# An encoder trunk in float32 halves: up-projections of eight in eleven chunks by seven block products, F tiles in three portions

## The chip, the cores and the metric

One core of a Trainium2 chip. The metric is the device time of one execution in microseconds (us); runs of one kernel lie within 0.1% of each other here. The engines are TensorE (PE; its weight loads are shown apart as PEld), VectorE (DVE), ScalarE (ACT), GpSimd (POOL) and SyncE (SP), which issues the loads of weights.

## What is computed

Two layers of an encoder over 512 tokens with a model width D of 1024. Each layer is an FFN, a token mixer (attention in a window, a pool over windows, gates) and another FFN. All is float32. The change is in the FFN:

```python
def swiglu(u, w1, w3, w2):
    return (jax.nn.silu(u @ w1) * (u @ w3)) @ w2
...
        h = h + 0.5 * swiglu(rms_norm(h, ffn1_norm[l]), ffn1_w1[l], ffn1_w3[l], ffn1_w2[l])
```

`w1` and `w3` are 1024 x 2816, `w2` is 2816 x 1024. So an FFN has K = 8 tiles of 128 in its two up-projections and 22 tiles of 128 hidden columns ("F tiles"), which come in 11 chunks of 256 columns.

## The kernel before

x lies with D on the partitions and the tokens along the free axis. A product keeps float32's bits by three parts: each operand is split into a high half (an exact copy in a shorter form, by ACT) and a low half (the difference, by DVE), and `mm3` adds high x high, high x low and low x high. Every part is a matmul of its own with its own weight load.

Weights come in pieces of 512 KB ([128, 1024] in SBUF): `do_load` lets SP fetch a piece into `raw` (3 buffers), `do_split` makes `wh` on ACT (L157) and `wl` on DVE (L158; 3 buffers each). Loads run four pieces ahead of use, splits two.

An FFN (`ffn`) goes through its F tiles in two portions, `HALVES = ((0, 12), (12, 22))`. For each chunk of 256 columns `pair` makes the products with `w1` and then with `w3`, over 8 K tiles, 2 column tiles, and 3 parts, each matmul with all 512 tokens as its moving columns: 96 matmuls. Then come `gate` (L376 to L380) and `gated` (L386), and `split_sb` splits the hidden tile for the down-projection. The inverse root of the norm, `r`, isn't in the operand `us`, so that the products may begin before it is known; `gate` multiplies it in twice. After each portion the down-projection runs over the portion's F tiles, four pairs of output tiles, and `residual` adds them to x (L359).

In the mixer attention is cut into small steps between the products of the gates: scores (L630, L631), softmax, transposes of probabilities (L677), their split (L679 on ACT, L680 on DVE), values (L693, L694). At the very end `natural` transposes x (L426) and `closing` makes the last down-projection with the tokens on the partitions.

The order on each engine is set by a scheduler from the program's order, its data and its buffers; PSUM has 8 banks of [128, 512], handed out in turn.

Of the kernel before, what the change touches and what calls it, by code (L numbers as in the profile page):

```python
# [38 lines left out]
PAD = 16  # L39
NEG = -1e30  # L40
LEAST = -3e38
KC = 4
HALVES = ((0, 12), (12, 22))
# [4 lines left out]
# Column layout of the packed vectors: the norm gains, biases, scales and sinks of each  # L48
# layer, and tables that depend on shapes alone.
# [22 lines left out]
def encoder_kernel(ctx, tc, x, vec, gfin, w1a, w3a, w2a, w_in, pool_w, w_ba, w_bp, w_out, w1b, w3b, w2b, out):  # L72
# [3 lines left out]
    act = ctx.enter_context(tc.tile_pool(name="act", bufs=56))  # L76
# [14 lines left out]
    def slot(dt=F32, n=512):  # L91
        return act.tile([P, n], dt, tag="slot", name=uniq("slot"))
# [22 lines left out]
    # the tensor engine's clock rises while the first data come in  # L115
# [16 lines left out]
    specs = []  # L132
    held = set()  # pieces that stay until the end, in slots of their own
    state = {"load": 0, "split": 0, "use": 0}
    raws, parts = {}, {}
    LOAD_AHEAD, SPLIT_AHEAD = 4, 2

    def piece(parts_of):
        specs.append(parts_of)

    def do_load(i):
        raw = wp.tile([P, 1024], F32, tag="raw", name=uniq("raw"), bufs=3)
        for lo, hi, shape, src in specs[i]:
            k, c = shape
            nc.sync.dma_start(out=raw[lo:hi, : k * c].rearrange("p (k c) -> p k c", k=k), in_=src)
        raws[i] = raw

    def do_split(i):
        raw = raws.pop(i)
        k, c = specs[i][0][2]  # L150
        n = k * c
# [3 lines left out]
        wh = wp.tile([P, 1024], F32R, tag="wh", name=uniq("wh"), bufs=3)  # L155
        wl = wp.tile([P, 1024], F32R, tag="wl", name=uniq("wl"), bufs=3)
# [7 lines left out]
    def ahead():  # L164
        while state["load"] < min(len(specs), state["use"] + LOAD_AHEAD):
            do_load(state["load"])
            state["load"] += 1
        while state["split"] < min(len(specs), state["use"] + SPLIT_AHEAD):
            do_split(state["split"])
            state["split"] += 1  # L170
# [17 lines left out]

    def plan_ffn(w1, w3, w2, first, last):
        for f0, f1 in HALVES:  # L190
            for c in range(f0 // 2, f1 // 2):
                if first and c == 0:
# [6 lines left out]
            if last and f0:  # L199
                for k0, k1 in ((f0, f1 - KC), (f1 - KC, f1)):  # L200
                    for e in range(2):
                        for k, n in ksteps(k0, k1, 2):
                            piece(wsrc(w2, k, n, e * 512, 512))
                            if k1 == f1:
                                held.add(len(specs) - 1)
# [36 lines left out]
    def pair(us, k0=0, k1=KD, between=None):  # L242
        """Two output tiles (256 columns of the weights) over the K tiles of `us`."""
# [13 lines left out]
    def turned(ps, half):  # L257
        """The transpose of an exact half."""
        nc.tensor.matmul(ps, lhsT=half, rhs=identr, start=True, stop=True)  # L259

    def split_sb(src, hi=None, lo=None):
        hi = slot(F32R) if hi is None else hi
        lo = slot(F32R) if lo is None else lo
# [11 lines left out]
    class Norm:  # L275
        """Sum of squares over the model dimension, tile by tile, then its inverse root."""
# [17 lines left out]
        def root(self, r, total, n):  # L294
            """r = (total / D + eps) ** -0.5, with a Newton step on the table's root."""
# [9 lines left out]
        def rows(self):  # L305
            """The inverse root of each token along the free axis, on every partition."""
# [7 lines left out]
        def cols(self):  # L314
            """The inverse root of each token on its partition, [P, NT]."""
# [526 lines left out]
```

## Time and profile before

| | |
|---|---|
| timed runs | 1999.99 us (median of 3; 1999.25 to 2000.25) |
| profiled execution, span from first to last instruction | 1997.6 us |
| what lies around the span, by the median of the runs | 2.4 us |
| matmuls | 9053 |
| busy: PE, DVE, ACT, POOL | 99%, 55%, 36%, 2% |
| DMA | 189.56 MB, mean 95 GB/s |

The profiled execution's own time isn't listed apart from the timed runs; its span is, and the runs' median stands beside it. A share of busy time is the union of an engine's instructions over the span; matmuls overlap each other, so PE's share says little by itself, and the distance between starts of equal matmuls says more. Idle time of an engine matters only where another one waits for its result.

### The profile page before, as it was taken

The numbers are of one execution on the slowest core, as the hardware profiler recorded it, in microseconds if no ns is written. First come the engines' busy times: TensorE is split into PE (matmuls) and PEld (weight loads), VectorE is DVE, ScalarE is ACT, GpSimd is POOL, SyncE is SP. The second block draws the span as 40 slices with busy tenths as digits, with TensorE's granted clock in tenths as the row PEclk, the third lists the DMA queues.
The fourth block names the chain that finished last, engine by engine and source line by source line (L and its number), as shares of the span: only waits on it lengthen the run. The fifth ranks groups of instructions, "written<-read, shape, count | busy, mean of one in ns | idle before, by whom it ended". The sixth has DMA issues, their size and how long they took to land.

```text
span 1997.6 us, 22600 instructions
## 1 busy us (share of the span) xinstructions
PE 1984.4 (99%) x9053; PEld 1650.2 (83%) x9053; DVE 1089.3 (55%) x1705; ACT 713.3 (36%) x1091; POOL 41.0 (2%) x48
## 2 busy tenths in 40 slices
PE   9999999999999999999999999999999999999998
PEld 7888888888888888888888888888888888888886
DVE  5753454477765654355456434545777647544444
ACT  4321233445553332222333212334466433222333
POOL 2000000020000000000000000000200000000000
PEclk9999999999999999999999999999999999999999
DMA  5333332322233233332333333333222333333332
GB/s 176 95 95 97 101 98 85 106 85 69 74 87 104 84 107 95 95 98 93 95 95 106 95 97 100 91 98 90 80 85 64 105 96 95 95 95 95 106 95 74
DMA packets 183467, 189.56 MB, mean 95 GB/s; under 512 B 6208, under 2 KB 176320, under 8 KB 183360
## 3 DMA queue, kind: packets, MB, share of 16 engines
q1 hardware_dynamic: 182496, 186.67, 31.6%
q8 instruction: 71, 1.16, 0.2%
q10 hardware_dynamic: 864, 1.43, 0.2%
q14 instruction: 36, 0.29, 0.0%
HBM read 185.98 MB, written 2.10 MB: 94 GB/s over the span
## 4 chain that ended last, share of the span: by engine, by line
PE 98%; ACT 0%; DVE 0%; issue 0%; ACTq 0%
PE bank L238 32%; PE bank L240 32%; PE bank L239 32%; PE bank L677 1%; PE bank L693 0%; PE bank L259 0%; PE bank L694 0%; PE bank L630 0%; PE bank L631 0%; ACT wh L157 0%; PE bank L426 0%; PE bank L308 0%; PE bank L309 0%; PE bank L320 0%; ACT tmp L460 0%; ACT slot L467 0%
## 5 line engine op out<-in xcount | busy, mean ns | idle before, releaser
L238 PE MATMUL bank<-slot,wh 128*128 128x512 f32 x2616 | 1024.0, 392 | 1.7 <-ACT wh L157 1.4
L240 PE MATMUL bank<-slot,wl 128*128 128x512 f32 x2616 | 1017.9, 389 | 2.3 <-DVE wl L158 2.3
L239 PE MATMUL bank<-slot,wh 128*128 128x512 f32 x2616 | 1018.6, 389 | 0.0
L157 ACT ACTIVATE wh<-raw 128x1024 fp32r<-128x1024 f32 (+1 forms) x356 | 368.4, 1035 | 1126.8 <-PE bank L239 786.8
L158 DVE TENSOR_TENSOR wl<-raw,wh 128x1024 fp32r<-128x1024 f32 (+1 forms) x356 | 427.6, 1201 | 483.8 <-ACT wh L157 482.8
L240 PEld LDWEIGHTS bank<-slot,wl 128*128 128x128 f32 x2616 | 491.0, 188 | 106.4 <-DVE wl L158 3.1
L238 PEld LDWEIGHTS bank<-slot,wh 128*128 128x128 f32 x2616 | 491.1, 188 | 102.1 <-ACT wh L157 3.8
L239 PEld LDWEIGHTS bank<-slot,wh 128*128 128x128 f32 x2616 | 491.3, 188 | 97.5
L386 DVE TENSOR_TENSOR tmp<-bank,tmp 128x512 f32<-128x512 f32 x88 | 60.0, 690 | 88.1 <-PE bank L240 88.1
L376 DVE TENSOR_TENSOR tmp<-bank,rrow 128x512 f32<-128x512 f32 x88 | 59.6, 690 | 83.9 <-PE bank L240 83.7
L379 DVE TENSOR_TENSOR tmp<-tmp,tmp 128x512 f32<-128x512 f32 x88 | 60.1, 687 | 23.6 <-ACT tmp L378 23.6
L265 DVE TENSOR_TENSOR slot<-tmp,slot 128x512 fp32r<-128x512 f32 x96 | 64.6, 704 | 6.2 <-ACT slot L264 6.2
L264 ACT ACTIVATE slot<-tmp 128x512 fp32r<-128x512 f32 x96 | 55.5, 617 | 22.2 <-DVE tmp L386 13.0
L238 PE MATMUL bank<-wh,slot 128*128 128x512 f32 (+1 forms) x176 | 61.8, 351 | 0.0
L240 PE MATMUL bank<-wh,slot 128*128 128x512 f32 (+1 forms) x176 | 61.7, 350 | 0.0
L239 PE MATMUL bank<-wl,slot 128*128 128x512 f32 (+1 forms) x176 | 61.7, 350 | 0.0
L359 DVE SCALAR_TENSOR_TENSOR x<-bank,x 128x512 f32<-128x512 f32 x56 | 38.2, 690 | 42.5 <-PE bank L240 42.5
L380 DVE TENSOR_TENSOR tmp<-tmp,rrow 128x512 f32<-128x512 f32 x88 | 60.2, 687 | 1.3
L378 ACT ACTIVATE tmp<-tmp 128x512 f32<-128x512 f32 x88 | 51.2, 618 | 17.1 <-DVE tmp L376 17.1
L654 ACT ACTIVATE s<-s,nm 128x256 f32<-128x256 f32 (+1 forms) x64 | 35.2, 551 | 30.2 <-DVE nm L649 30.0
L272 DVE SCALAR_TENSOR_TENSOR slot<-x,vt,slot 128x512 fp32r<-128x512 f32 x48 | 40.4, 845 | 1.6 <-ACT slot L271 1.6
L240 PEld LDWEIGHTS bank<-wh,slot 128*128 128x128 f32 x176 | 33.3, 189 | 4.4
(124 smaller groups left out, 969.9 us busy)
## 6 DMA issues: line engine op xcount, KB each, us to landing
raw<-in_ffn_w_dram SPq DMA_DIRECT2D x254, 512.0 KB, 3.7
raw<-in_w_in_dram SPq DMA_DIRECT2D x52, 512.0 KB, 3.8
raw<-in_w_out_dram SPq DMA_DIRECT2D x16, 512.0 KB, 3.5
raw<-in_ffn_w_dram SPq DMA_DIRECT2D x20, 256.0 KB, 2.9
raw<-in_w_branch_pool_dram SPq DMA_DIRECT2D x8, 512.0 KB, 3.5
raw<-in_w_branch_attn_dram SPq DMA_DIRECT2D x16, 256.0 KB, 4.0
x<-in_x_dram SPq DMA_DIRECT2D x8, 256.0 KB, 4.9
out_dram<-slot SPq DMA_DIRECT2D x4, 256.0 KB, 2.1
```

Of the source, the lines that this page charges most:

```text
L157: nc.scalar.activation(wh[:, :n], raw[:, :n], AF.Copy)
L158: nc.vector.tensor_tensor(out=wl[:, :n], in0=raw[:, :n], in1=f(wh[:, :n]), op=ALU.subtract)
L238: nc.tensor.matmul(ps, lhsT=lh, rhs=rh, start=start, stop=False)
L239: nc.tensor.matmul(ps, lhsT=lh, rhs=rl, start=False, stop=False)
L240: nc.tensor.matmul(ps, lhsT=ll, rhs=rh, start=False, stop=stop)
L264: nc.scalar.activation(hi, src, AF.Copy)
L265: nc.vector.tensor_tensor(out=lo, in0=src, in1=f(hi), op=ALU.subtract)
L376: nc.vector.tensor_tensor(out=a, in0=p[t], in1=r, op=ALU.mult)
L378: nc.scalar.activation(s, a, AF.Sigmoid)
L379: nc.vector.tensor_tensor(out=a, in0=a, in1=s, op=ALU.mult)
L380: nc.vector.tensor_tensor(out=a, in0=a, in1=r, op=ALU.mult)
L386: nc.vector.tensor_tensor(out=ta[t], in0=p[t], in1=ta[t], op=ALU.mult)
```

## The change

In the first portion, now 6 F tiles (3 chunks), a chunk is computed as before. In the other two, 8 tiles (4 chunks) each, a chunk's two up-projections are taken together as one 2 x 2 block product: weights in blocks (`w1`, `w3`) x (lower, upper half of K), tokens in two halves of 256. By Winograd's form of Strassen's scheme seven products of blocks stand for eight; each is over 4 K tiles with 256 moving columns. Sums of weight blocks are made on DVE (`combine` in `plan_seven`), sums of operand blocks once an FFN (`factors`), with the norm's `r` and gain multiplied in, so that `silu` needs no `r`. The seven products (`seven`) share three PSUM banks: ACT copies a bank out (`kept`), and a later product adds to what is in it. All three portions' down-projections are as before, of 6, 8 and 8 K tiles. Buffers are laid out anew: `raw` has 9, `wh` and `wl` 4 each, `act` 23 of 4 KB in place of 56 of 2 KB; in the mixer the scores lie in a `raw` buffer and a `tmp`. The transposes of x at the end (`natural`) stand together before `closing`.

```diff
-HALVES = ((0, 12), (12, 22))
+LEAD = 9
+PORTIONS = ((0, 6), (6, 14), (14, 22))
...
+    def plan_seven(w1, w3, c0):
...
+        event(i - 8, fetch, "21", w3, 0)
+        event(i - 8, fetch, "22", w3, KC)
+        event(i - 7, fetch, "11", w1, 0)
+        event(i - 6, fetch, "12", w1, KC)
+        event(i - 4, combine, "s3", "11", ALU.subtract, "21")
+        event(i - 3, combine, "21", "21", ALU.add, "22")
+        event(i - 3, ready, 0, "11")
+        event(i - 2, combine, "11", "11", ALU.subtract, "21")
+        event(i - 1, ready, 1, "12")
+        event(i, ready, 2, "11")
+        event(i, combine, "12", "12", ALU.add, "11")
+        event(i + 1, ready, 3, "21")
+        event(i + 2, ready, 4, "s3")
+        event(i + 3, ready, 5, "12")
+        event(i + 4, ready, 6, "22")
...
+        for f0, f1 in PORTIONS:
+            last = f1 == KF
+            gs = []
+            for c in range(f0 // 2, f1 // 2):
+                if f0:
+                    seven(forms, gs)
...
+                else:
+                    ta = gate(pair(us, between=steps))
+                    gated(pair(us, between=steps), ta, gs)
...
+    def factors(g, r):
...
+            nc.vector.scalar_tensor_tensor(
+                out=b[n][:, k % KC * HT : (k % KC + 1) * HT], in0=xs[k][:, c], scalar=col(g, k), in1=r[:, c],
+                op0=ALU.mult, op1=ALU.mult,
+            )
...
+        def ready(n):
+            src, hi, lo = b.pop(n), big(), big()
+            nc.scalar.activation(hi, src, AF.Copy)
+            nc.vector.tensor_tensor(out=lo, in0=src, in1=f(hi), op=ALU.subtract)
...
+    def seven(forms, gs):
...
+            for k in range(KC):
+                for t in range(2):
+                    c = slice(t * P, (t + 1) * P)
+                    o = ps[:, t * HT : (t + 1) * HT]
+                    last = k == KC - 1
+                    nc.tensor.matmul(
+                        o, lhsT=wh[:, k, c], rhs=bh[:, k, :], start=start and k + t == 0, stop=False, skip_group_check=True
+                    )
+                    nc.tensor.matmul(o, lhsT=wh[:, k, c], rhs=bl[:, k, :], start=False, stop=False, skip_group_check=True)
+                    nc.tensor.matmul(o, lhsT=wl[:, k, c], rhs=bh[:, k, :], start=False, stop=last, skip_group_check=True)
+
+        def kept(ps):
+            v = tmp()
+            nc.scalar.activation(v, ps, AF.Copy)
+            return v
...
+        x, y, z = bank(), bank(), bank()
+        product(x, "11", True)
+        p1 = kept(x)
+        product(z, "21", True)
+        a1 = tmp()
+        nc.vector.tensor_tensor(out=a1, in0=z, in1=p1, op=ALU.add)
+        silu(a1)
+        product(x, "t2", False)
+        u2 = kept(x)
+        product(y, "t1", True)
+        p5 = kept(y)
+        product(x, "12", False)
+        u3 = kept(x)
+        b2 = p5
+        nc.vector.tensor_tensor(out=b2, in0=u3, in1=p5, op=ALU.add)
+        product(y, "22", False)
+        a2 = u2
+        nc.vector.tensor_tensor(out=a2, in0=y, in1=u2, op=ALU.add)
+        silu(a2)
+        product(x, "t4", False)
+        nc.vector.tensor_tensor(out=a1, in0=x, in1=a1, op=ALU.mult)
+        hidden(0, a1)
+        nc.vector.tensor_tensor(out=b2, in0=b2, in1=a2, op=ALU.mult)
+        hidden(1, b2)
```

Three places show how the order moves; rows are in the order in which an engine takes them, with the changed kernel's own line numbers in its rows.

**DVE in a chunk.** Before, in the first FFN's first portion (L158 splits a weight piece, L376 to L386 gate, L265 splits a hidden tile; one more L265 and L158 end the chunk's 14 rows):

```order
L376 TENSOR_TENSOR tmp_158_875<-bank_150_813,rrow_74_404 128x512
L376 TENSOR_TENSOR tmp_160_881<-bank_151_814,rrow_74_404 128x512
L379 TENSOR_TENSOR tmp_158_875<-tmp_158_875,tmp_159_877 128x512
L158 TENSOR_TENSOR wl_166_892<-raw_152_815,wh_165_891 128x1024
L380 TENSOR_TENSOR tmp_158_875<-tmp_158_875,rrow_74_404 128x512
L379 TENSOR_TENSOR tmp_160_881<-tmp_160_881,tmp_161_883 128x512
L380 TENSOR_TENSOR tmp_160_881<-tmp_160_881,rrow_74_404 128x512
L158 TENSOR_TENSOR wl_169_922<-raw_155_845,wh_168_921 128x1024
L386 TENSOR_TENSOR tmp_158_875<-bank_162_887,tmp_158_875 128x512
L386 TENSOR_TENSOR tmp_160_881<-bank_163_888,tmp_160_881 128x512
L158 TENSOR_TENSOR wl_178_964<-raw_164_889,wh_177_963 128x1024
L265 TENSOR_TENSOR slot_171_951<-tmp_158_875,slot_170_950 128x512
```

In the changed kernel, the end of a chunk of its second portion (L196 splits a weight block, L238 is a sum of weight blocks, L598 to L606 and L575 gate, L582 splits a hidden tile):

```order
L238 TENSOR_TENSOR raw_206_1172<-raw_206_1172,raw_197_1128 128x1024
L196 TENSOR_TENSOR wl_227_1363<-raw_210_1204,wh_226_1362 128x1024
L598 TENSOR_TENSOR tmp_219_1295<-tmp_224_1330,tmp_219_1295 128x512
L238 TENSOR_TENSOR raw_210_1204<-raw_210_1204,raw_206_1172 128x1024
L601 TENSOR_TENSOR tmp_215_1263<-bank_202_1165,tmp_215_1263 128x512
L196 TENSOR_TENSOR wl_236_1406<-raw_206_1172,wh_235_1405 128x1024
L575 TENSOR_TENSOR tmp_215_1263<-tmp_215_1263,tmp_225_1359 128x512
L604 TENSOR_TENSOR tmp_211_1230<-bank_201_1164,tmp_211_1230 128x512
L606 TENSOR_TENSOR tmp_219_1295<-tmp_219_1295,tmp_215_1263 128x512
L196 TENSOR_TENSOR wl_240_1439<-raw_197_1128,wh_239_1438 128x1024
L582 TENSOR_TENSOR big_200_1163<-tmp_211_1230,big_199_1162 128x2x256
L582 TENSOR_TENSOR big_200_1163<-tmp_219_1295,big_199_1162 128x2x256
```

A chunk has gone from 14 rows (4 of 1024 columns) to 20 (11 of 1024: 7 splits and 4 sums); the gating rows L598, L601, L604 and L606 stand among splits and sums that belong to the next chunk.

**ACT in a chunk.** Before, at the same place (L157 copies a piece's high half, L378 is the sigmoid, L264 a hidden tile's high half):

```order
L157 ACTIVATE wh_156_847<-raw_143_773 128x1024
L157 ACTIVATE wh_165_891<-raw_152_815 128x1024
L378 ACTIVATE tmp_159_877<-tmp_158_875 128x512
L378 ACTIVATE tmp_161_883<-tmp_160_881 128x512
L157 ACTIVATE wh_168_921<-raw_155_845 128x1024
L157 ACTIVATE wh_177_963<-raw_164_889 128x1024
L264 ACTIVATE slot_170_950<-tmp_158_875 128x512
L264 ACTIVATE slot_172_955<-tmp_160_881 128x512
```

In the changed kernel (L195 copies a block's high half, L569 is `kept`, the copy of a bank, L574 the sigmoid):

```order
L195 ACTIVATE wh_213_1235<-raw_187_1031 128x1024
L569 ACTIVATE tmp_207_1198<-bank_201_1164 128x512
L195 ACTIVATE wh_216_1265<-raw_179_966 128x1024
L574 ACTIVATE tmp_212_1232<-tmp_211_1230 128x512
L195 ACTIVATE wh_220_1297<-raw_167_908 128x1024
L569 ACTIVATE tmp_215_1263<-bank_201_1164 128x512
L195 ACTIVATE wh_222_1302<-raw_206_1172 128x1024
L569 ACTIVATE tmp_219_1295<-bank_202_1165 128x512
L195 ACTIVATE wh_226_1362<-raw_210_1204 128x1024
L569 ACTIVATE tmp_224_1330<-bank_201_1164 128x512
L195 ACTIVATE wh_235_1405<-raw_206_1172 128x1024
L574 ACTIVATE tmp_225_1359<-tmp_215_1263 128x512
```

Each copy of a bank stands behind the copy of a weight block, and the one ahead of `tmp_225_1359`'s sigmoid reads a sum that DVE makes.

**PE in the mixer.** The values of the third head in the first layer, with what each row waits for. Before:

```order
L693 MATMUL bank_736_3914<-slot_692_3761,slot_492_2927 128x256 [waits DVE_49]
L694 MATMUL bank_736_3914<-slot_693_3762,slot_492_2927 128x256
L693 MATMUL bank_736_3914<-slot_695_3768,slot_492_2927 128x256
L694 MATMUL bank_736_3914<-slot_696_3769,slot_492_2927 128x256
L693 MATMUL bank_736_3914<-slot_698_3782,slot_492_2927 128x384
L694 MATMUL bank_736_3914<-slot_699_3783,slot_492_2927 128x384
L693 MATMUL bank_736_3914<-slot_701_3796,slot_492_2927 128x384
L694 MATMUL bank_736_3914<-slot_702_3797,slot_492_2927 128x384
```

And now (L894 and L895 are L693 and L694 of before; `big` holds the probabilities of one or two blocks of keys):

```order
L894 MATMUL bank_762_4662<-big_728_4519,big_549_3706 128x256 [waits DVE_49,Activation_49]
L895 MATMUL bank_762_4662<-big_728_4519,big_549_3706 128x256
L894 MATMUL bank_762_4662<-big_728_4519,big_549_3706 128x256 [waits Activation_49]
L895 MATMUL bank_762_4662<-big_728_4519,big_549_3706 128x256
L894 MATMUL bank_762_4662<-big_731_4537,big_549_3706 128x384 [waits Activation_49]
L895 MATMUL bank_762_4662<-big_731_4537,big_549_3706 128x384
L894 MATMUL bank_762_4662<-big_733_4550,big_549_3706 128x384 [waits Activation_49]
L895 MATMUL bank_762_4662<-big_733_4550,big_549_3706 128x384
```

Before, the row of values waits once, for DVE; now four of its rows wait for ACT's copy as well. Over the eight heads of a layer 14 of the 32 first rows of a block waited for ACT, and 25 do now.

## Rows read from the trace of the kernel before

**Rows 1.** The page: busy time, share, xinstructions by engine; granted clock in slices
```profile
PE 1984.4 (99%) x9053; PEld 1650.2 (83%) x9053; DVE 1089.3 (55%) x1705; ACT 713.3 (36%) x1091; POOL 41.0 (2%) x48
...
PEclk9999999999999999999999999999999999999999
```

**Rows 2.** The page: the chain that ended last, by engine and line
```profile
PE 98%; ACT 0%; DVE 0%; issue 0%; ACTq 0%
PE bank L238 32%; PE bank L240 32%; PE bank L239 32%; PE bank L677 1%; PE bank L693 0%; PE bank L259 0%; PE bank L694 0%; PE bank L630 0%; PE bank L631 0%; ACT wh L157 0%; PE bank L426 0%; PE bank L308 0%; PE bank L309 0%; PE bank L320 0%; ACT tmp L460 0%; ACT slot L467 0%
```

**Rows 3.** Timeline of PE: start us, us, line, out<-in, form, count
```profile
632.73 0.39 PE L240 MATMUL bank<-slot,wl 128*128 128x512 f32 x1
...
662.20 0.39 PE L238 MATMUL bank<-slot,wh 128*128 128x512 f32 x1
```

**Rows 4.** Timeline of PE in the k/v projection, 256 columns
```profile
392.75 0.28 PE L238 MATMUL bank<-wh,slot 128*128 128x256 f32 x1
...
403.79 0.28 PE L240 MATMUL bank<-wh,slot 128*128 128x256 f32 x1
```

**Rows 5.** Timeline of PE's weight loads (PEld) in the k/v projection
```profile
399.84 0.19 PEld L238 LDWEIGHTS bank<-wh,slot 128*128 128x128 f32 x1
399.96 0.19 PEld L239 LDWEIGHTS bank<-wl,slot 128*128 128x128 f32 x1
```

**Rows 6.** Busy time in the stretch of the k/v projection
```profile
core 0: us, PE busy (x) PEld busy (x) DVE busy (x) ACT busy (x) POOL busy (x), PEclk, DMA share, GB/s
392.30:403.90 11.60, 11.60 (x98) 11.60 (x98) 9.54 (x42) 8.51 (x19) 0.15 (x2) 1.00 0.24 65
```

**Rows 7.** Timeline of DVE, back to back
```profile
66.23 0.69 DVE L386 TENSOR_TENSOR tmp<-bank,tmp 128x512 f32<-128x512 f32 x1
66.83 1.22 DVE L158 TENSOR_TENSOR wl<-raw,wh 128x1024 fp32r<-128x1024 f32 x1
67.97 0.69 DVE L265 TENSOR_TENSOR slot<-tmp,slot 128x512 fp32r<-128x512 f32 x1
```

**Rows 8.** Groups by line: xcount | busy us, mean ns | idle before
```profile
L158 DVE TENSOR_TENSOR wl<-raw,wh 128x1024 fp32r<-128x1024 f32 x334 | 410.6, 1229 | 481.4 <-ACT wh L157 480.5
L157 ACT ACTIVATE wh<-raw 128x1024 fp32r<-128x1024 f32 x334 | 354.5, 1061 | 1092.0 <-PE bank L239 756.2 <-issue 296.1 <-PE bank L240 34.2
...
L386 DVE TENSOR_TENSOR tmp<-bank,tmp 128x512 f32<-128x512 f32 x88 | 60.0, 690 | 88.1 <-PE bank L240 88.1
...
L378 ACT ACTIVATE tmp<-tmp 128x512 f32<-128x512 f32 x88 | 51.2, 618 | 17.1 <-DVE tmp L376 17.1
...
L272 DVE SCALAR_TENSOR_TENSOR slot<-x,vt,slot 128x512 fp32r<-128x512 f32 x48 | 40.4, 845 | 1.6 <-ACT slot L271 1.6
...
L679 ACT ACTIVATE slot<-bank 128x384 fp32r<-128x384 f32 x32 | 14.7, 490 | 3.5 <-PE bank L677 2.6 <-PE bank L259 0.7
...
L428 ACT ACTIVATE slot<-bank 128x512 f32<-128x512 f32 x8 | 4.3, 584 | 0.0
```

**Rows 9.** Timeline of all engines, around a read of a finished PSUM bank
```profile
75.30 0.39 PE L240 MATMUL bank<-slot,wl 128*128 128x512 f32 x1
...
75.73 0.69 DVE L386 TENSOR_TENSOR tmp<-bank,tmp 128x512 f32<-128x512 f32 x1 [1.08 <-PE bank L240]
```

**Rows 10.** Timeline of ACT, back to back (row two: two instructions)
```profile
76.18 1.06 ACT L157 ACTIVATE wh<-raw 128x1024 fp32r<-128x1024 f32 x1 [3.81 <-PE bank L239]
77.15 1.14 ACT L264 ACTIVATE slot<-tmp 128x512 fp32r<-128x512 f32 x2
```

**Rows 11.** Waits: engine, line <- waited for: us in total, times, longest us
```profile
PEld bank L238 <- ACT wh L157: 3.8, 5, 1.8
...
PE bank L240 <- DVE wl L158: 2.3, 2, 1.3
...
PEld bank L693 <- ACT slot L679: 0.4, 2, 0.2
```

**Rows 12.** Busy time in the first layer's mixer (columns as in Rows 6)
```profile
369.70:670.30 300.60, 300.59 (x1479) 254.10 (x1479) 193.35 (x412) 144.42 (x272) 14.59 (x18) 1.00 0.30 87
```

More of the change, by code (lines that the diff above doesn't have):

```diff
@@ L39 @@
 PAD = 16
+HT = S // 2
+ACTS = 23
+RAWS = 9
+SPLITS = 4
 NEG = -1e30
@@ L162, in do_split, with upto @@
         )
[L164 to L170, printed above, removed]
+    def upto(i):
+        while state["event"] <= i:
+            for fn, args in events.pop(state["event"], []):
+                fn(*args)
+            state["event"] += 1
     def weights():
         i = state["use"]
-        ahead()
+        upto(i)
         state["use"] += 1
-        ahead()
         return parts.pop(i)
@@ L198, in plan_ffn @@
                 plan_pair(w3, c * 256)
-            if last and f0:
+            if last and f1 == KF:
                 for k0, k1 in ((f0, f1 - KC), (f1 - KC, f1)):
@@ L330, in encoder_kernel @@
         if k % 2 == 0:
-            while state["load"] < (2, 2, 3, 3)[k // 2]:
-                do_load(state["load"])
-                state["load"] += 1
+            for i in range((2, 2, 3, 3)[k // 2]):
+                do_load(i, uses[i])
     def opening():
@@ L342, in opening @@
                 if j == 0:
-                    ahead()
+                    upto(state["use"])
             w = [weights(), weights()]
@@ L387, in gated @@
                 gs.append(split_sb(ta[t]))
-        for hf, (f0, f1) in enumerate(HALVES):
-            last = hf == len(HALVES) - 1
+        for f0, f1 in PORTIONS:
+            last = f1 == KF
             gs = []
             for c in range(f0 // 2, f1 // 2):
-                if c == 0:
+                if f0:
+                    seven(forms, gs)
+                elif c == 0:
                     late = ups or [pair(us), pair(us)]
-                    continue
-                pa = pair(us)
-                if late:
+                elif c == 1:
+                    pa = pair(us)
                     norm.split()
@@ L400, in ffn @@
                     gated(late[1], gate(late[0]), gs)
-                    late = []
-                ta = gate(pa)
-                gated(pair(us), ta, gs)
-                if last and gain is None and c - f0 // 2 < NT:
-                    natural(c - f0 // 2)
+                    ta = gate(pa)
+                    gated(pair(us), ta, gs)
+                    forms, steps = factors(g, r)
+                else:
+                    ta = gate(pair(us, between=steps))
+                    gated(pair(us, between=steps), ta, gs)
             if last and gain is None:
+                for t in range(NT):
+                    natural(t)
                 closing(gs, f0, f1)
@@ L411, in ffn @@
             for d in range(KD // 2):
-                ps = pair(gs, f0, f1)
+                ps = pair(gs, f0, f1, None if f0 else steps)
+                if not f0 and d == KD // 2 - 1:
+                    steps(True)
                 for t in range(2):
@@ L516, in mixer @@
                     mm3(pk[t][:, :256], uh[:, c], ul[:, c], wh[:, j, :], wl[:, j, :], first, last)
-        kn = slot()
-        vs = [slot(F32R) for _ in range(KVH)]
+        kn = tmp()
+        vs = two()
         for t in range(NT):
```

176 lines of the change are left out of this document (134 added, 42 removed).

## The prediction

> **What bounds the kernel now.** Read the busy shares first: TensorE (PE) is busy 99% of the span, VectorE (DVE) 55%, ScalarE (ACT) 36%, and the clock digit is 9 in every slice, so the granted clock is at its upper level (2.4 GHz) throughout [rows 1]. A busy PE isn't yet a bound PE, because its matmuls are pipelined. So read the chain that ended last next: 98% of it is PE, and the three lines of `mm3` carry 96% [rows 2]. PE waits for almost nothing, so what the change does to the time is what it does to the spacing and number of matmuls, plus whatever waits it puts in. Spacing is read from starts, not from durations, which overlap (0.39 us each): 131 matmuls with 512 columns start from 632.73 to 662.20, so (662.20 - 632.73)/130 = 226.7 ns [rows 3]. The kernel already has a stretch of 256-column matmuls, the k/v projection: 93 of them from 392.75 to 403.79, or (403.79 - 392.75)/92 = 120.0 ns [rows 4].
>
> **Matmuls.** A chunk had 96 matmuls of 512 columns: 96 x 226.7 ns = 21.76 us. It gets 7 products x 4 K tiles x 2 tiles x 3 parts = 168 of 256 columns: 168 x 120.0 ns = 20.16 us. An eighth of the chunk would be 2.72 us; 1.60 is left, because half the columns cost more than half the time (120.0 against 113.4 ns). Eight chunks in each of four FFNs: 32 x 1.60 = **51.3 us saved**. The rest of the matmuls keep their number: a third portion only cuts the same 22 K tiles of the down-projection otherwise.
>
> What could spoil the 120 ns is the weight load, since a load is now needed every 120 ns and takes 0.19 us [rows 5]. In the k/v stretch loads take the same 0.19 us and yet start 0.12 us apart, side by side with each other and with the matmuls [rows 5], while DVE was busy for 9.54 and ACT for 8.51 of 11.60 us [rows 6], so neither loads nor other engines' traffic stretched the spacing there. I take 120.0 ns. The Trainium skill, in "TensorE: Matmul & The Clock Gate" (Part 3, The mechanism), says that a weight load overlaps matmuls in flight only when its row group differs; these loads take all rows, so by that rule the loads would stand in line, and the sum would turn into a large loss (a rival below). The rows speak against it.
>
> **VectorE.** In steady state a chunk had 4 splits of 1024 columns and 10 operations of 512; by the new order it has 7 splits and 4 sums of 1024, and 9 of 512. What one occupies is again start to start: 0.60 us for 512 columns, from PSUM too, and 1.14 for 1024 [rows 7]. So 4 x 1.14 + 10 x 0.60 = 10.6 us before and 11 x 1.14 + 9 x 0.60 = 17.9 us now, of 20.16. The upper bound is full durations, 11 x 1.229 + 9 x 0.690 = 19.7 us [rows 8]. Either fits, closely. The cover is the lead: with four split buffers the split of a product may begin when the product four back is done, and is needed three products (3 x 24 x 0.120 = 8.6 us) later. About 1.5 us of this is the copy and subtraction themselves, some queueing goes off too; I count two products, 5.8 us. A portion is four chunks, so DVE could fall 1.4 us behind in each, to 21.6 us a chunk, before PE waits. Then the down-projection (192 x 0.2267 = 43.5 us, with 8 splits and 8 residuals, 13.9 us) lets it recover. Cost taken: 0.
>
> **The factors of each FFN** are 16 scalings of 256 columns (nearest row 845 ns for 512 [rows 8]; half, 0.4 us), 4 sums and 7 splits: 16 x 0.4 + 11 x 1.14 = 18.9 us of DVE. They stand in the last chunk and the down-projection of the first portion, 21.8 + 144 x 0.2267 = 54.4 us, in which DVE also has 10.6 us of gating, 12 us of pieces and residuals and 4.6 us of the next chunk's sums: 46 of 54. Hidden; uncovered it would cost at most the 18.9 us a time.
>
> **Banks that PE takes again.** This is a new wait. Product 3 adds to the bank of product 1 after ACT has copied it out, and so for four copies a chunk, 128 in all, with one product (24 x 0.120 = 2.88 us) between. By the order a split copy stands ahead of each on ACT, released by the same product. A reader starts 0.43 us after the start of the last 512-column matmul (75.30 to 75.73), which is 0.39 of its duration and 0.04 [rows 9]; for 256 columns that is 0.28 + 0.04 - 0.12 = 0.20 us after the next product's start. Then the split copy 0.97 (76.18 to 77.15 [rows 10]) and the copy-out 0.58 [rows 8]: 1.75 of 2.88 us. Margin 1.1 us; cost taken 0.
>
> **Splits at the head of an FFN.** PE's loads wait for a split copy five times, 3.8 us in all, the longest 1.8 in the opening; the other four, one an FFN after its norm, are (3.8 - 1.8)/4 = 0.5 us each [rows 11]. With four split buffers for three these copies stand a product earlier: **2.0 us saved**. The opening's two waits for a subtraction (2.3 us [rows 11]) may go as well, as nine raw buffers let loads run on; taken as 0, bound 2.3.
>
> **Mixer.** Only buffers change, but the scheduler answers with another order: 25 instead of 14 value products per layer wait for a copy of transposed probabilities, as the fenced rows show, and their low halves and reused banks do likewise; I count some 20 more close waits per layer. The nearest row is such a pair at the end of today's attention, 0.2 us each [rows 11]: 20 x 2 x 0.2 = **8 us lost**. Bounds: 0, and 0.5 us each (a copy of 384 columns, 0.49 us [rows 8], not hidden at all), 20 us.
>
> **End.** The transposes of x now stand together ahead of the last down-projection, eight banks, each freed by a copy of 0.58 us [rows 8]: from 0 to 8 x 0.58 = 4.7 us. Copies and transposes overlap; **1 us lost**.
>
> Sum on the profiled execution: 1997.6 - 51.3 - 2.0 + 8 + 1 = 1953.3 us span. The median of the timed runs, 1999.99, is 2.4 above the span, which I keep: **1956 us**.
>
> **Rivals.**
> *DVE becomes the bound.* For it: 17.9 to 19.7 of 20.16 us, and in its row stand four operations that wait for PE and ACT's results, each of which can idle it. With 19.7 plus four waits of 0.35 (a result's 0.20 and some) a chunk takes 21.1, the lead is used up within a portion, and 32 x (21.76 - 21.1) = 21 us are saved: 1986. Against: start-to-start costs, and the lead.
> *The copy-outs hold PE, and it is slower.* ACT runs its row in order. If it lags by one split copy and one sigmoid (0.97 + 0.62 [rows 8]), a copy-out ends at 1.75 + 1.59 = 3.34 us, 0.46 late, at each of 128 places: 59 us lost against 51 saved, 2015. It decides from 51.3/128 = 0.40 us per copy-out, that is, from a lag of 1.5 us. For it: ACT's split copies wait for DVE's sums, so a late DVE delays ACT. Against: the 1.1 us of margin, and that ACT has 11 of 20 us of work (7 x 0.97 + 4 x 0.58 + 4 x 0.5).
> *The mixer pays more*: 40 places at 0.9 us (copy and subtraction bare) lose 36 us: 1984. For it: the order; against: such waits of PE come to 0.4 us today [rows 11].
> *Weight loads don't overlap at 256 columns*: 168 x 0.19 = 31.9 us a chunk, 32 x (31.9 - 21.76) = 325 us lost in place of the 51 saved, 2332. Against it stand [rows 5], loads 0.12 us apart. By the Trainium skill's rule named above this is what would come.
>
> **Chances.** PE stays the bound as summed: 0.77, from 1944 (mixer and end free, opening gains 2.3) to 1972 (mixer 20, end 4.7). DVE bound 0.10; mixer 0.05; copy-outs 0.06; loads 0.02. Nine tenths of the first are 0.69, so the range reaches to the price of the DVE and mixer cases, which brings in some 0.10 more: **1944 to 1987**. A measurement of this kernel tells about 0.2% (4 us) from no change. Slower are the last two cases without their mildest form, 0.07; same 0.02; faster 0.91.
>
> **What the profile will show.** Right: PE still 98% of the chain; in a chunk the 256-column lines 120 ns apart, chunk starts 20.2 us apart; DVE near 89% busy there; PE's waits for copy-outs about nil; the loads' 0.5 us waits gone. Wrong: matmul spacing at 0.19 us; PE's idle time before the subtraction line of the splits (DVE), or before the first matmul of a product with ACT's copy-out as releaser; a mixer longer by over 10 us than today's 300.6 us [rows 12]. What would make the forecast wrong is above all an ACT or DVE row that can't keep its order's pace.

## The result and the profile after

The changed kernel takes **1953.41 us** (median of 4 runs, 1953.15 to 1953.44) against 1999.62 us for the kernel before (4 runs). The ratio is 0.9769, with a 95% interval from 0.9755 to 0.9783: 46.2 us faster. The forecast was 1956, between 1944 and 1987. The profiled execution has a span of 1951.6 us where I had summed 1953.3.

First the page of the changed kernel: busy time, share of the span and instructions by engine, then the chain that ended last. These answer to [rows 1] and [rows 2].

```profile
PE 1937.0 (99%) x11357; PEld 1719.5 (88%) x11357; DVE 1408.9 (72%) x2039; ACT 913.5 (47%) x1345; POOL 40.3 (2%) x48
...
PE 97%; DVE 1%; ACT 1%; issue 0%
PE bank L311 20%; PE bank L313 20%; PE bank L312 20%; PE bank L565 11%; PE bank L564 11%; PE bank L561 11%; PE bank L875 1%; PE bank L828 1%; PE bank L332 0%; PE bank L829 0%; PE bank L895 0%; PE bank L894 0%; DVE big L881 0%; ACT wh L195 0%; PE bank L620 0%; DVE wl L196 0%
```

VectorE went from 55% to 72% of the span and ScalarE from 36% to 47%, and neither of them came onto the chain: it is still TensorE almost alone, now with a third of its time in the 256-column lines L561, L564 and L565. What is new on the chain is small, 1% each of DVE (L881, L196) and ACT (L195).

Now the place where the gain was forecast. The rows are TensorE's timeline at the first and after the last matmul of a portion of four chunks by seven products (start us, us, line, tiles, form).

```profile
108.02 0.28 PE L561 MATMUL bank<-big,wh 128*128 128x256 f32 x1
108.13 0.28 PE L564 MATMUL bank<-big,wh 128*128 128x256 f32 x1
...
188.53 0.28 PE L565 MATMUL bank<-big,wl 128*128 128x256 f32 x1
188.65 0.40 PE L311 MATMUL bank<-big,wh 128*128 128x512 f32 x1
```

From 108.02 to 188.65 stand 4 x 168 = 672 matmuls: 80.63/672 = 120.0 ns, 20.16 us a chunk. All eight portions of the program take 80.63 or 80.64 us. The forecast rate, read off the k/v projection [rows 4], held to the last digit.

Next the busy time in stretches of the changed kernel, one layer: the rest of the first portion with its down-projection, the first portion by seven products, its down-projection, the second such portion, and the mixer (the last row answers to [rows 12]).

```profile
core 0: us, PE busy (x) PEld busy (x) DVE busy (x) ACT busy (x) POOL busy (x), PEclk, DMA share, GB/s
...
42.09:108.02 65.93, 65.93 (x291) 54.37 (x290) 62.40 (x85) 29.79 (x36) 0.00 (x0) 1.00 0.26 74
108.02:188.65 80.63, 80.63 (x673) 80.63 (x672) 70.28 (x77) 46.01 (x58) 0.00 (x0) 1.00 0.41 125
188.65:232.20 43.55, 43.55 (x194) 36.05 (x193) 24.18 (x26) 9.53 (x10) 0.00 (x0) 1.00 0.21 61
232.20:312.83 80.63, 80.63 (x673) 80.63 (x672) 65.02 (x72) 45.90 (x58) 0.00 (x0) 1.00 0.41 125
356.34:660.42 304.08, 302.08 (x1479) 253.45 (x1479) 194.23 (x412) 144.17 (x272) 14.58 (x18) 1.00 0.28 83
```

TensorE is busy without a gap in the first four. DVE is busy for 87% and 81% of the two portions, and for 62.40 of 65.93 us in the stretch where the factors are made: nearly full, and TensorE doesn't wait. The mixer is the only one of the five with a gap: 304.08 us with 302.08 busy, where [rows 12] have 300.60.

The whole difference by stage follows from one marker, the first matmul of each norm's sum (L308 before, L381 after), which starts six times in each trace:

| From norm to norm | Before, us | After, us | Difference |
|---|---|---|---|
| start to first norm | 42.32 | 42.09 | -0.2 |
| FFN of layer 1, q and k/v projection | 372.50 | 359.37 | -13.1 |
| rest of the mixer, layer 1 | 255.53 | 259.01 | +3.5 |
| second FFN of layer 1 | 360.08 | 346.91 | -13.2 |
| FFN of layer 2, q and k/v projection | 372.48 | 359.36 | -13.1 |
| rest of the mixer, layer 2 | 255.58 | 259.05 | +3.5 |
| last FFN to the end of the span | 339.11 | 325.81 | -13.3 |

Unrounded they add up to -46.0, the difference of the spans. Each FFN gives 8 x 1.60 = 12.8 by the chunks and some 0.35 beside them; each mixer takes 3.5 back.

### The profile page after: what moved, and what is told of

Read it like the earlier page. It is cut to its first block, busy times and chain, and to the rows that moved or that the text cites. A ratio compares the mean times of both kernels' runs of the same rounds, so it can differ in the third digit from the quotient of the medians.

```text
span 1951.6 us, 27947 instructions
## 1 busy us (share of the span) xinstructions
PE 1937.0 (99%) x11357; PEld 1719.5 (88%) x11357; DVE 1408.9 (72%) x2039; ACT 913.5 (47%) x1345; POOL 40.3 (2%) x48
## 4 chain that ended last, share of the span: by engine, by line
PE 97%; DVE 1%; ACT 1%; issue 0%
PE bank L311 20%; PE bank L313 20%; PE bank L312 20%; PE bank L565 11%; PE bank L564 11%; PE bank L561 11%; PE bank L875 1%; PE bank L828 1%; PE bank L332 0%; PE bank L829 0%; PE bank L895 0%; PE bank L894 0%; DVE big L881 0%; ACT wh L195 0%; PE bank L620 0%; DVE wl L196 0%
## 5 line engine op out<-in xcount | busy, mean ns | idle before, releaser
L195 ACT ACTIVATE wh<-raw 128x1024 fp32r<-128x1024 f32 (+1 forms) x454 | 470.4, 1036 | 818.8 <-PE bank L312 417.5
L196 DVE TENSOR_TENSOR wl<-raw,wh 128x1024 fp32r<-128x1024 f32 (+1 forms) x454 | 543.7, 1199 | 280.9 <-ACT wh L195 274.3
L311 PE MATMUL bank<-big,wh 128*128 128x512 f32 x1544 | 606.5, 394 | 4.0 <-DVE big L881 3.4
L313 PE MATMUL bank<-big,wl 128*128 128x512 f32 x1544 | 602.0, 390 | 0.9 <-DVE wl L196 0.9
L312 PE MATMUL bank<-big,wh 128*128 128x512 f32 x1544 | 602.3, 390 | 0.0
L565 PE MATMUL bank<-big,wl 128*128 128x256 f32 x1792 | 507.1, 283 | 0.0
L564 PE MATMUL bank<-big,wh 128*128 128x256 f32 x1792 | 507.1, 283 | 0.0
L561 PE MATMUL bank<-big,wh 128*128 128x256 f32 x1792 | 507.1, 283 | 0.0
L311 PEld LDWEIGHTS bank<-big,wh 128*128 128x128 f32 x1544 | 290.4, 188 | 63.0 <-DVE big L881 4.7
L313 PEld LDWEIGHTS bank<-big,wl 128*128 128x128 f32 x1544 | 290.3, 188 | 62.3 <-DVE wl L196 1.3
L561 PEld LDWEIGHTS bank<-big,wh 128*128 128x128 f32 x1792 | 344.0, 192 | 0.3
L564 PEld LDWEIGHTS bank<-big,wh 128*128 128x128 f32 x1792 | 344.0, 192 | 0.3
L565 PEld LDWEIGHTS bank<-big,wl 128*128 128x128 f32 x1792 | 344.0, 192 | 0.0
L312 PEld LDWEIGHTS bank<-big,wh 128*128 128x128 f32 x1544 | 290.8, 188 | 55.3
L238 DVE TENSOR_TENSOR raw<-raw,raw 128x1024 f32<-128x1024 f32 x128 | 156.0, 1219 | 1.5
L569 ACT ACTIVATE tmp<-bank 128x512 f32<-128x512 f32 x128 | 74.2, 580 | 0.0
L311 PE MATMUL bank<-wh,big 128*128 128x512 f32 (+1 forms) x160 | 55.7, 348 | 0.0
L313 PE MATMUL bank<-wh,big 128*128 128x512 f32 (+1 forms) x160 | 55.5, 347 | 0.0
L574 ACT ACTIVATE tmp<-tmp 128x512 f32<-128x512 f32 x64 | 40.2, 627 | 23.0 <-DVE tmp L601 18.0
L575 DVE TENSOR_TENSOR tmp<-tmp,tmp 128x512 f32<-128x512 f32 x64 | 43.7, 683 | 0.0
```

What stands on the lines that cost most here:

```text
L195: nc.scalar.activation(wh[:, :n], raw[:, :n], AF.Copy)
L196: nc.vector.tensor_tensor(out=wl[:, :n], in0=raw[:, :n], in1=f(wh[:, :n]), op=ALU.subtract)
L238: nc.vector.tensor_tensor(out=t[out], in0=t[a], in1=t[b], op=op)
L311: nc.tensor.matmul(ps, lhsT=lh, rhs=rh, start=start, stop=False)
L312: nc.tensor.matmul(ps, lhsT=lh, rhs=rl, start=False, stop=False)
L313: nc.tensor.matmul(ps, lhsT=ll, rhs=rh, start=False, stop=stop)
```

## Experiments

Two theories were to be told apart at each place. On the gain: that the seven products are worth just their matmuls, since all that they add on VectorE and ScalarE is hidden, against the view that some of it shows. On the mixer: that the smaller number of `big` tiles makes the loss, against that scores and attention outputs now hold buffers of the weights.

### Eight products, all else as changed

```diff
-                if f0:
-                    plan_seven(w1, w3, c * 256)
-                    continue
...
                 if f0:
-                    seven(forms, gs)
+                    ta = gate(pair(us))
+                    gated(pair(us), ta, gs)
...
-                    forms, steps = factors(g, r)
```

> The changed kernel's portions, buffers and mixer, but every chunk by eight products of 512 columns, without factors and sums of weights. If the seven products are worth just their matmuls and the factors, sums and copy-outs cost TensorE nothing: 1953.4 + 32 x 1.60 = 2004.6 us, and the FFN stages else unchanged. Rival: the extra VectorE and ScalarE work stretches TensorE's work somewhere; then this lies below 2004.6 by what it costs, 5 us or more to be seen (the upper bound that I had for uncovered factors is 4 x 18.9 us).

Measured: 2004.61 us, ratio 1.0027 (1.0017 to 1.0037): what was expected. Portions and buffers without the seven products make the kernel 0.3% slower, and the products are worth 2004.61 - 1953.41 = 51.2 us, as their matmuls alone give. Sums, factors and copy-outs together cost TensorE nothing that can be measured. By the norm markers (42.12, 414.25, 673.26, 1032.93 here) the first FFN with the projections takes 372.13 us and the second 359.67, each 0.4 less than before, and the mixer between them 259.01, as in the changed kernel: so the 0.35 an FFN and the mixer's loss come with the new portions and buffers, not with the products.

### The mixer: how many `big` tiles

Here is ScalarE's timeline in the changed kernel where TensorE waits longest (in brackets: the time that it was idle before, and for what).

```profile
468.48 0.59 ACT L900 ACTIVATE tmp<-bank 64x512 f32<-64x512 f32 x1
470.93 0.63 ACT L902 ACTIVATE raw<-tmp 64x512 fp32r<-64x512 f32 x1 [1.86 <-DVE tmp L901]
471.58 0.60 ACT L803 ACTIVATE big<-bank 128x512 fp32r<-128x512 f32 x1
472.20 1.06 ACT L195 ACTIVATE wh<-raw 128x1024 fp32r<-128x1024 f32 x1
473.17 1.02 ACT L880 ACTIVATE big<-bank 128x256 fp32r<-128x256 f32 x3
```

And TensorE in the same kernel:

```profile
473.17 0.39 PE L313 MATMUL bank<-big,wl 128*128 128x512 f32 x1
475.03 0.50 PE L311 MATMUL bank<-big,wh 128*128 128x512 f32 x1 [1.47 <-DVE big L881]
```

The three copies of transposed probabilities (L880) read three banks whose seven transposes started between 466.16 and 468.38. They begin at 473.17 only, behind an output of attention (L902) for which ScalarE itself waited 1.86 us, and a split copy. VectorE's subtraction (L881) follows each copy and frees the bank, and the product that wants the bank waits 1.47 us. That is a wait for a bank, behind a copy that stands late in ScalarE's row. The weight loads' list of waits in this mixer (us in total, times, longest) begins with it:

```profile
PEld bank L311 <- DVE big L881: 2.3, 2, 1.9
PEld bank L895 <- DVE big L881: 1.0, 2, 0.7
PEld bank L894 <- ACT big L880: 1.0, 4, 0.3
```

The experiment changes the number of tiles these copies write to, at the cost of raw buffers, which hold as much:

```diff
-ACTS = 23
-RAWS = 9
+ACTS = 25
+RAWS = 7
```

> Changed kernel with 25 big tiles instead of 23 and 7 raw buffers instead of 9. Theory A: the mixer's loss (3.48 us a layer, all of it in the attention stretch) comes from too few big tiles. Copies of transposed probabilities get a free tile late in the scheduler's order and so stand behind other work in ACT's row; with 25 tiles the attention stretch returns from 242.2 to about 238.7 us a layer, 7.0 us in all: 1946.4 us. Rival B: scores and attention outputs hold raw buffers that weights then lack; 7 raw buffers make that worse: over 1953.4. Rival C: two pairs of halves sharing one big tile is the cause, whatever the number of tiles: 1953.4.

> 24 big tiles, 8 raw buffers. Theory A: a part of the 7.0 us comes back, some three quarters by the number of close waits in the order: about 1948 us, and between 1946.4 and 1953.4 in any case. Rivals B and C: 1953.4 or more.

> The changed kernel with 7 raw buffers and its own 23 big tiles: the control of the run with 25 and 7. Theory A (big tiles alone make the mixer's loss): as the changed kernel, 1953.4 us, attention stretch 242.2 us a layer. Rival (fewer raw buffers, and so other loads, gave the gain there): about 1947.

Measured: 1946.75 us with 25 and 7 (ratio 0.9739, 0.9725 to 0.9752), 1948.09 with 24 and 8 (0.9744, 0.9731 to 0.9758), 1953.54 with 23 and 7 (0.9772, 0.9756 to 0.9788). From the second to the third norm marker, the mixer's 259.01 us became 256.28 with 24 tiles and 255.67 with 25 (before: 255.53), and stayed at 259.10 in the control. So the number of `big` tiles it is; rivals B and C fall. The same copies in the kernel with 25 tiles, where the mixer starts 0.1 us earlier and this place, by L900, lies 1.1 us earlier:

```profile
467.35 0.59 ACT L900 ACTIVATE tmp<-bank 64x512 f32<-64x512 f32 x1
467.96 1.04 ACT L880 ACTIVATE big<-bank 128x256 fp32r<-128x256 f32 x3
469.80 0.63 ACT L902 ACTIVATE raw<-tmp 64x512 fp32r<-64x512 f32 x1 [0.79 <-DVE tmp L901]
```

They stand ahead of L902 and begin 5.2 us earlier, and of the waits above one is left in this mixer:

```profile
PEld bank L895 <- DVE big L881: 0.5, 1, 0.5
```

TensorE's own order is nearly the same: by the two traces, taken row for row, 112 of 11,357 matmuls are of another line or form, all in the mixers. A few of them stand at this place, where two products of values come earlier with 25 tiles; the copies that TensorE waited for moved in ScalarE's row. The kernel with 25 tiles and 7 raw buffers is **the best version of this study**, 6.7 us below the changed kernel.

### The fourth split buffer

```diff
-ACTS = 23
-SPLITS = 4
+ACTS = 25
+SPLITS = 3
```

> Three split buffers (as in the kernel before) instead of four, 25 big tiles, 9 raw buffers; to be read against the run with 25 big tiles and 7 raw. Theory: the fourth split buffer is worth the waits at the heads of the FFNs alone (0.3 to 0.5 us each): 1946.4 + 1 to 2 = 1947.4 to 1948.4 us, since VectorE, busy 18.1 of 20.16 us a chunk, keeps pace with one product less of lead. Rival: the lead of the fourth buffer is what lets VectorE keep pace through its waits in order; then chunks grow over 20.16 us, and 10 us or more are lost: 1956 or more.

Measured: 1950.34 us (ratio 0.9755, 0.9742 to 0.9769), 3.6 above the kernel with four split and seven raw buffers. Neither number was met. The chunks by seven products keep 80.63 us a portion, so the rival falls: VectorE keeps pace with one product less of lead. The loss is in the first portion of each FFN, as the busy time from its norm to the first chunk by seven products shows, here with three split buffers (65.93 us with four):

```profile
42.03:108.79 66.76, 66.53 (x292) 54.20 (x290) 62.86 (x85) 29.76 (x36) 0.00 (x0) 1.00 0.28 79
```

Its weight loads wait for two things (us in total, times, longest):

```profile
PEld bank L311 <- ACT wh L195: 3.4, 5, 1.4
...
PEld bank L311 <- ACT big L337: 2.3, 4, 0.6
```

The first is the five waits that [rows 11] have, one in the opening and one of 0.49 us in each FFN, in nearly the same size; with four buffers the one in the opening is left. The second, four waits for the gated tiles of the first portion, I hadn't counted. Together they cost 0.83 us an FFN, 3.3 in all; the other 0.3 us stand in the mixers.

### How much room VectorE has

With `EXTRA` of 1, in the first kernel for the sums `s3` and `12` alone, in the second for all four:

```diff
         def combine(out, a, op, b):
...
+            for _ in range(EXTRA):
+                nc.vector.tensor_tensor(out=t[out], in0=t[a], in1=t[a], op=ALU.max)
             nc.vector.tensor_tensor(out=t[out], in0=t[a], in1=t[b], op=op)
```

> The changed kernel with two more VectorE operations of 1024 columns in each chunk by seven products: a maximum of a weight tile with itself ahead of two of the four sums, the output as before. VectorE's use of a chunk goes from 18.1 to 18.1 + 2 x 1.14 = 20.4 of 20.16 us. Theory (lead of two products, 5.8 us): 0.2 us behind a chunk, about 1 us in a portion of four, hidden: 1953.4 us. Rival (VectorE is at its bound already through its waits in order): up to 32 x 2.28 = 73 us lost, 2026.

> Such an extra operation ahead of each of the four sums: 22.7 of 20.16 us a chunk, 10.2 us behind in a portion of four chunks. With a lead of two products (5.8 us) that is made up in each down-projection, 8 x 4.4 = 35 us lost: 1988. With three products (8.6 us) 13 us lost: 1966. With no lead 32 x 2.54 = 81 us lost: 2034. The scheduler's order of TensorE changes in some 380 rows here.

Measured: 1955.03 us with two (ratio 0.9779, 0.9765 to 0.9794) and 1995.43 with four (0.9980, 0.9971 to 0.9990). With two, all eight portions keep 80.63 or 80.64 us. Of the 1.6 us, 1.2 stand ahead of the first norm (43.30 instead of 42.09), in the opening, before any chunk by seven products, and 0.3 in the first mixer; why the new order costs time there isn't shown. With four the portions grow, and the two of an FFN by different amounts:

```profile
109.19:198.40 89.21, 83.42 (x674) 81.19 (x673) 87.86 (x93) 44.34 (x59) 0.00 (x0) 1.00 0.36 109
241.94:324.43 82.49, 81.39 (x673) 80.78 (x672) 77.87 (x84) 44.36 (x58) 0.00 (x0) 1.00 0.39 120
```

DVE is busy for 87.86 of 89.21 us in the first: there it is the bound. The first portion inherits VectorE work from the stretch of the factors, 70.28 us busy against 65.02 in the changed kernel, and so has 5 us less room. The second also loses time, with VectorE at 77.87 of 82.49 us. The mean over both, (8.58 + 1.86)/2 = 5.2 us a portion, is near the 4.4 expected from a lead of two products, but by luck: the expectation took all portions as alike. How the delay reaches TensorE is seen in the waits of this kernel:

```profile
ACT wh L196 <- DVE raw L241: 146.3, 40, 6.4
...
PE bank L564 <- ACT tmp L572: 14.6, 26, 1.1
...
PE bank L564 <- ACT wh L196: 11.9, 8, 1.7
```

TensorE names ScalarE (the copy-outs, here L572, and the split copies, L196), not VectorE: ScalarE's split copies wait for VectorE's sums (L241; 146.3 us in all, 10.0 in the changed kernel), and the copy-outs stand behind them. That is the link the slower rival of the prediction needed; its time here, 1995.43, is about where the gain is used up.

### How much room the copy-outs have

In the changed kernel a copy-out (L569) ends at 152.90, and the bank's next matmul starts at 154.09, its load at 153.97. ScalarE, TensorE and the load:

```profile
151.35 1.06 ACT L195 ACTIVATE wh<-raw 128x1024 fp32r<-128x1024 f32 x1 [0.39 <-PE bank L564]
152.32 0.58 ACT L569 ACTIVATE tmp<-bank 128x512 f32<-128x512 f32 x1
...
154.09 0.28 PE L561 MATMUL bank<-big,wh 128*128 128x256 f32 x1
...
153.97 0.19 PEld L561 LDWEIGHTS bank<-big,wh 128*128 128x128 f32 x1
```

The experiment repeats the copy, three times in the first kernel and four (`range(4)`) in the second:

```diff
         def kept(ps):
             v = tmp()
-            nc.scalar.activation(v, ps, AF.Copy)
+            for _ in range(3):
+                nc.scalar.activation(v, ps, AF.Copy)
```

> Each copy-out of a bank that TensorE takes again is made three times instead of once, the output as before: some 2 x 0.5 = 1.0 us later, of a margin that the changed kernel's trace shows as 1.19 us (copy ends at 152.90, the bank is taken again at 154.09). Order of TensorE as in the changed kernel. Theory: hidden, 1953.4 us. Rival (ScalarE in order lags more than that here and there): 0.4 us at 128 places would be 51 us, 2004.

> Each such copy-out made four times: 1.5 us later, 0.3 more than the margin. Theory: 0.3 x 128 = 40 us lost, 1993, less as far as the scheduler's new order of TensorE (it differs in some 1,100 rows) puts other matmuls into the gap. Rival (the margin is wider than the copy alone shows, say a product more): 1953.4.

Measured: 1968.73 us with three copies (ratio 0.9848, 0.9833 to 0.9863), 2024.97 with four (1.0129, 1.0114 to 1.0144). I expected 1953.4 and 1993: both were missed, in the same direction. The cause of one part is in ScalarE's timeline with three copies: they take 1.84 us together, since these repeats into one tile don't overlap: they start 0.61 and 0.63 us apart and last 0.58 to 0.60 each.

```profile
152.31 1.06 ACT L195 ACTIVATE wh<-raw 128x1024 fp32r<-128x1024 f32 x1 [0.41 <-PE bank L564]
153.27 1.84 ACT L570 ACTIVATE tmp<-bank 128x512 f32<-128x512 f32 x3
```

A copy more is 1.84 - 0.58 = 1.26 us for two, not 1.0. TensorE and its load after it, in the same kernel:

```profile
154.99 0.28 PE L565 MATMUL bank<-big,wl 128*128 128x256 f32 x1
155.17 0.38 PE L561 MATMUL bank<-big,wh 128*128 128x256 f32 x1
155.39 0.28 PE L564 MATMUL bank<-big,wh 128*128 128x256 f32 x1
...
155.17 0.19 PEld L561 LDWEIGHTS bank<-big,wh 128*128 128x128 f32 x1
```

The copies end at 155.11 and the load starts at 155.17, 0.06 us later. It is the load that waits, and the load stands 0.12 us ahead of its matmul when nothing is late (153.97 and 154.09 above). So the margin is 154.09 - 0.12 - 0.06 - 152.90 = 1.0 us, not 1.19. The copies overran it by some 0.25 us. The place costs (155.39 - 154.99) - 2 x 0.12 = 0.16 us of this, and where the rest is made up isn't shown; over the kernel (1968.73 - 1953.41)/128 = 0.12. With four copies it is 71.6/128 = 0.56 us. From the third copy to the fourth the loss grows by 0.44 of a copy's 0.63; with four the scheduler's order of TensorE is another one too, so I don't read a slope from it.

### The factors with less cover

```diff
-ACTS = 23
-RAWS = 9
+ACTS = 25
+RAWS = 7
...
-PORTIONS = ((0, 6), (6, 14), (14, 22))
+PORTIONS = ((0, 4), (4, 14), (14, 22))
...
-    for _ in range(len(todo) if rest else 1 if n < 16 or n % 2 else 0):
+    for _ in range(len(todo) if rest else 2):
```

> Portions of 4, 10 and 8 F tiles, seven products in 9 of 11 chunks, factors made at two steps per K tile in a down-projection of 21.8 us; 25 big tiles, 7 raw buffers. Matmuls: 4 x 1.60 = 6.4 us less than the 1946.75 of that buffer setting. By the busy time that the changed kernel's trace shows for VectorE in this stretch (62.4 us) less the chunk that leaves it (10.6 us and some 3 us of splits of the down-projection), 49 us have to fit into 65.9 - 21.8 - 10.9 = 33 us: 16 us too many, of which lead and slack of the next chunks take perhaps a half: 8 us lost in each FFN, 1946.75 - 6.4 + 32 = 1972 us, between 1955 and 2004. Rival (the factors' time was never tight, they hide anywhere): 1940.4.

Measured: 2006.33 us (six runs from 2002.75 to 2009.03, ratio 1.0034, 1.0022 to 1.0046; the trace is of the shortest), over the upper end of what I gave, and slower than the kernel before. The FFNs are 13 to 15 us longer than with 25 tiles and the old portions. TensorE's own busy time and clock show two holes, one ahead of the down-projection and one in the first chunk by seven products (columns as above):

```profile
53.80:60.90 7.10, 0.03 (x1) 0.00 (x0) 7.07 (x12) 4.73 (x7) 0.00 (x0) 0.66 0.26 76
60.90:62.00 1.10, 1.07 (x2) 0.50 (x2) 1.10 (x3) 0.58 (x1) 0.00 (x0) 0.50 0.00 0
...
65.00:66.00 1.00, 1.00 (x3) 0.79 (x3) 1.00 (x3) 0.09 (x1) 0.00 (x0) 0.50 0.00 0
...
95.00:97.00 2.00, 0.12 (x1) 0.12 (x2) 2.00 (x4) 0.00 (x0) 0.00 (x0) 1.00 0.00 0
97.00:99.00 2.00, 2.00 (x10) 2.00 (x11) 2.00 (x2) 0.92 (x1) 0.00 (x0) 0.52 0.00 0
```

The second hole is the one that I had summed: VectorE is busy throughout, first with the factors, and TensorE waits for a split that stands behind them. The first is another: the down-projection wants gated tiles at once, and with no chunk between, the norm's root and the gating stand bare, 7.1 us. So the third chunk of the first portion covers two things, the factors and the gating. And after each hole TensorE works at 0.50 of the clock, 1.2 GHz, which I hadn't counted at all: in the first the clock falls within the hole (0.66 is its mean there) and stays low from 60.9 to about 66 us, in the second it is low from about 97 to 100.5. By the starts of the matmuls against the regular 226.7 and 120.0 ns, the first FFN loses 7.3 us in the first hole, 5 in the holes of the first chunk and 4.4 to the lower clock (2.8 and 1.6), against 1.6 gained by its ninth chunk.

### Halving once more

One of the three parts of a product; the two others are cut in the same way:

```diff
-                    nc.tensor.matmul(o, lhsT=wh[:, k, c], rhs=bl[:, k, :], start=False, stop=False, skip_group_check=True)
+                    for q in (slice(0, P), slice(P, 2 * P)):
+                        nc.tensor.matmul(o[:, q], lhsT=wh[:, k, c], rhs=bl[:, k, q], start=False, stop=False, skip_group_check=True)
```

> Each matmul of the seven products cut into two of 128 columns with the same weights, the output as before: 336 instead of 168 a chunk. If the weight loads set a floor, by the rows of the transposes by matmul in the changed kernel (8 of 128 columns, each with weights of its own, in 0.84 us: 0.105 each): 336 x 0.105 = 35.3 us a chunk, 32 x 15.1 = 484 us more, 2437 us. If columns set the spacing (512 in 226.7 ns and 256 in 120.0 give 13.3 ns plus 0.417 a column, 66.7 for 128): 22.4 us a chunk, 32 x 2.24 = 72 us more, 2025 us. Loads in line at 0.19 us each: 63.8 us a chunk, 3350 us.

Measured: 2509.57 us (one run). TensorE's timeline in such a chunk, two matmuls a row:

```profile
130.13 0.39 PE L568 MATMUL bank<-big,wl 128*128 128x128 f32 x2
130.35 0.39 PE L562 MATMUL bank<-big,wh 128*128 128x128 f32 x2
130.58 0.39 PE L566 MATMUL bank<-big,wh 128*128 128x128 f32 x2
```

That is (130.58 - 130.13)/4 = 0.112 us a matmul: half the columns of the 256-column form, and almost its time. Columns don't set the spacing any more; something of 0.11 us a matmul with its load does. The floor was read slightly too low from the transposes (0.105), 2437 for 2510. Every matmul has a load of its own in the trace (10,752 of each in these lines), also where two in a row use the same weights. Which of load and matmul makes the floor these rows don't tell, and no run here separates them.

## Why the prediction was right, step by step

- **Matmuls, -51.3**: 51.2 by the run with eight products, 120.0 ns by the rows. The 256-column form lies just above the floor of the experiment with 128 columns (0.112), so it was a near thing: the same products cut into 128 columns take 2509.57 us, 556 more.
- **Weight loads**: they overlap each other and the matmuls, as [rows 5] had it: loads of 0.19 us start 0.12 apart throughout the portions, and PEld is busy in all of the 80.63 us without holding PE. The sentence in the Trainium skill, "TensorE: Matmul & The Clock Gate" (Part 3, The mechanism), that overlap wants different row groups, taken alone, would have given the 2332 us of the rival; this trace disagrees with it. The same section of the Trainium skill also lets a load go ahead when it is into the background weight buffer; whether these loads go there no run shows, but by that sentence they may overlap, as they do.
- **VectorE, 0**: right. In a chunk of the changed kernel it was taken for some 18.1 of 20.16 us (148.41 to 168.57, less 2.0 idle), 17.9 by the sum. The bound was 2 to 4 operations a chunk away: two more cost the chunks nothing, four cost 42 us.
- **Factors, 0**: right, with less room than summed. The factors took 20.0 us of VectorE (18.9 by the sum), but all its work in that stretch was 52 of 54 us, not 46:

```profile
53.60:108.02 54.42, 54.42 (x241) 45.06 (x240) 52.34 (x76) 23.97 (x31) 0.00 (x0) 1.00 0.25 73
```

The cover was needed: of the 17 us that the first FFN lost with a chunk less of it, some 5 are holes behind the factors, the rest the bare gating and the lower clock.
- **Copy-outs, 0**: right. The order of ScalarE and the 1.75 us were as summed (1.69 by the rows, 152.90 - 151.21); the margin is 1.0 us rather than 1.1, because the load has to be early.
- **Splits at the head of the FFNs, -2.0**: -1.4 (4 x 0.35). The loads' list has one wait for a split copy in place of five, as forecast, yet each FFN gained 0.35 us and not 0.5. The step that was sized wrongly took a load's wait for TensorE's: in the kernel before, the load that starts at 65.87 had waited 0.49 us, and the matmuls around it start as follows:

```profile
65.42 0.39 PE L239 MATMUL bank<-slot,wh 128*128 128x512 f32 x1
65.87 0.50 PE L238 MATMUL bank<-slot,wh 128*128 128x512 f32 x1
66.21 0.63 PE L240 MATMUL bank<-slot,wl 128*128 128x512 f32 x2
```

That is (66.21 - 65.42) - 2 x 0.2267 = 0.34 us of TensorE's time. Against three buffers in the same new portions the fourth is worth 3.3.
- **Opening, 0**: -0.2.
- **Mixer, +8**: +7.0, but by another way. I had counted 20 pairs of short waits a layer at 0.2 us each. The trace shows a few: by the list of waits of layer 1 above the loads wait 2.3 us in two places for L881's banks, 1.0 in two for L881 and 1.0 in four for L880. The order pointed at the right stage and the right cause (a copy too close to its use), and the size agrees by luck: fewer waits, each longer.
- **End, +1**: the last FFN gained as much as the others (-13.3), so nothing was lost there.

From 1953.3 to the 1951.6 us of the span it is thus -1.1 for the end, -1.0 for the mixer, -0.2 for the opening and +0.6 for the heads. The DVE and copy-out rivals did not happen, but the experiments put their thresholds close: between 2.3 and 4.6 us more of VectorE a chunk, and about 1 us more of ScalarE a copy-out.

## What to carry to other kernels

Fewer products with smaller tiles paid here because the smaller matmul still cost nearly by its columns: read its spacing from a stretch of the kernel that has that form already, and find the floor (here 0.112 us) before going further. When engines beside the bound fill up, ask what lead each has and test it with harmless extra operations: the knee, not the busy share, tells how close the next change may go. And when a change takes buffers from another stage, look at the rows of the engines that write those buffers: two tiles (8 KB a partition, taken from raw buffers that weren't needed) gave 6.7 us back.

## What the runs showed of the hardware

In the kernel with portions of 4, 10 and 8, the granted clock fell within a hole of 7.1 us in TensorE's work and was 0.50 (1.2 GHz) until about 66 us; near 97 it was so again after two us, 95 to 97, with 0.12 us of work. In the changed kernel it was 1.00 in every stretch shown above. A matmul of 128 columns with a weight load of its own came every 0.112 us in the cut products (every 0.105 in eight transposes by matmul, L332, from 418.26 to 419.10 in the changed kernel), one of 256 columns every 0.120. And in these traces a wait for a PSUM bank falls on the weight load ahead of the matmul: the bank was needed 0.12 + 0.06 = 0.18 us earlier than the matmul's row shows.
